# A hybrid mLSTM / attention / expert layer on one core: the products of each weight tile ordered by its high and low part

## The chip, the core and the metric

The kernel runs on one core of a Trainium2 chip. Its engines are TensorE (PE in the profile, with PEld for its weight loads), VectorE (DVE), ScalarE (ACT), GpSimd (POOL) and SyncE (SP), which issues most of the transfers. The metric is the device time of one execution in microseconds.

## The reference, cut to what matters

One layer for 256 latent tokens and 256 context tokens, width 2048, in float32:

```
h, hc   = modulate(rmsnorm(x)), modulate(rmsnorm(ctx))         # shifts and scales from c @ w_mod
q,k,v,z,gates,qa,ka,va,ga,gb = split(h @ w_in + b_in)          # the same for hc
y_m     = mLSTM in both directions (8 heads x 128), gated by z
y_d     = differential attention (8 heads)
x       = x + g1 * ((sig(ga) * (y_m @ w_pa) + sig(gb) * (y_d @ w_pb)) @ w_out)
h2      = modulate(rmsnorm(x))
s       = (h2 @ w_pq) . sub_keys   ->   top 16 of 16 x 16 for each of 8 heads   ->   idx, softmax g
act     = gelu(h2 . expert_u[idx])                             # 16384 experts
x       = x + g2 * sum(g * act * expert_v[idx])
out     = rmsnorm(x) * final_norm_w
```

## The kernel before, in words

All large products run in a rounded float32 format (`F32R`). To keep float32 accuracy each operand is split in two parts: a high part, the operand cast to that format, and a low part, the operand less its high part. A product of two operands is then three: high by high, activation-high by weight-low, activation-low by weight-high. `PASS` lists the three as pairs (part of the first operand, part of the second); index 0 is the high part and 1 the low one.

Weights come in tiles of 128 x 1024 (512 KB). `stage` brings one: a transfer into `raw` on SP's queue (line 117), a cast to `hi` on ACT (line 133) and a subtraction to `lo` (line 136) on DVE, or, in part of the kernel, every fourth one on POOL. The three tiles of each kind go round in rings of three buffers, and staging runs two to three tiles ahead (`look`). `take()` hands the next pair `hl = (hi, lo)` to its user. The users of the pairs are these:

- `token_part` (line 278): token-major blocks, where the activations are stationary and the weights move, 512 columns a product. Four token tiles (latent and context: `vm`, `va`) or two (`zm`, the output projection from `mgT`). Eight tiles make a block.
- `chan_part` (line 289): channel-major blocks, where the weights are stationary and 256 tokens move. With `n` = 2 both latent and context tokens (`hL`, `hC`; four accumulators: `km`, `ka`), with `n` = 1 the latent ones (two accumulators of two halves: `qa`, `qm`, gates, branch projections from `yT` and the like, and the query projection from `h`).
- `u_pair` (lines 1225 to 1228; both its products stand in the profile as line 93, the helper `mp_`): the expert stage, 256 tiles of `expert_u`. For each of eight chunks one product of `hi` with both parts of h2 (512 columns), and one of `lo` with its high part (256 columns), both into `s`.

The accumulators `acc` of the projections come from a pool of four PSUM buffers. A block that is done is emptied at once by ACT or DVE (lines 490, 500, 615, 665 and so on), and the next block's accumulator in the same buffer waits for that. Between blocks, `pump` advances generators with the other work: conv, mLSTM, attention, top-16 search, gate maps, lists of experts. In the expert stage, the two results of a pair are reduced on DVE (line 1634) and activated on ACT (line 1635), ahead of later casts in these engines' own order.

Last comes the sum over rows of `expert_v`. Some rows are used as float32 directly (groups of 32 tokens, `v<-vraw,w`), others are split (`split`, lines 1524 and 1526) and multiplied in `v_part`:

```
def v_part(hl, ins, t, hf_):
    for sa, sb in PASS:
        for c in range(2):
            mp_(out_acc[t][hf_ * 2 + c], lhsT=ins[sa], rhs=hl[sb][:, c * 512:(c + 1) * 512],
                start=False, stop=False, skip_group_check=True)
```

Products issued by `mm` are placed by a scheduler, which follows the order of the code where operands are ready by its own reckoning and moves others forward otherwise. Those issued by `mp_` keep the order of the code. On the chip each engine runs its fixed list in order.

Of the kernel before, what the change touches and what calls it, by code (L numbers as in the profile page):

```python
# [31 lines left out]
P = 128  # L32
D = 2048
T = 256
# [52 lines left out]
def build(tc, a, dump=None):  # L87
    nc = tc.nc
    mm = nc.tensor.matmul


    def mp_(*args, **kw):
        tc.keep_in_program_order(mm(*args, **kw))  # L93
# [21 lines left out]
    def load(src, pool, bufs, queue=nc.sync):  # L115
        r = pool.tile([P, 1024], F32, name="raw", tag="raw", bufs=bufs)
        d = queue.dma_start(r, src)  # L117
        if by_four[0]:
            tc.keep_in_program_order(d)
        return r  # L120
# [40 lines left out]
    def take():  # L161
        while len(ahead) < look[0]:
            src = next(todo, None)
            ahead.append(None if src is None else stage(src))
        return ahead.pop(0)
# [45 lines left out]
    def m_tile():  # L211
        return psM.tile([P, 512], F32, name="m", tag="m")
# [19 lines left out]
        return t if tok is None else t[:, tok * P:(tok + 1) * P]  # L232


    PASS = ((0, 0), (0, 1), (1, 0))
    ALL = (0, 1, 2, 3)
    back = []

# [13 lines left out]
    def pump(rate, ahead=2, beside=0):  # L252
        for i, (q, r) in enumerate(((front, ahead), (back, rate), (side, beside))):
            credit[i] += r if q else 0
            while credit[i] > 0.99:
                credit[i] -= 1
                step(q)
# [14 lines left out]
            step(back)  # L272

    def token_part(acc, hl, kp, lhs, first, last):
        for ti in range(len(acc)):
            for k2 in range(2):
                for i, (sa, sb) in enumerate(PASS):
                    mm(acc[ti], lhsT=lhs(sa, ti, 2 * kp + k2), rhs=hl[sb][:, k2 * 512:(k2 + 1) * 512],  # L278
                       start=first and k2 == 0 and i == 0, stop=last and k2 == 1 and i == 2)

    def chan_part(acc, hl, kp, rhs, n, first, last):

        for c in range(4):
            for k2 in range(2):
                k = 2 * kp + k2
                for i, (sa, sb) in enumerate(PASS):
                    for g in range(n):
                        w = (c if n == 1 else g) % 2
                        mm(acc[c][:, g * T:(g + 1) * T],  # L289
                           lhsT=hl[sb][:, k2 * 512 + c * P:k2 * 512 + (c + 1) * P], rhs=rhs(sa, g, k),  # L290
                           start=first and k2 == 0 and i == 0 and w == 0,
                           stop=last and k2 == 1 and i == 2 and w == 1, skip_group_check=True)

    def h_lhs(s, t, k):
        return hT(s, t // 2, k, t % 2)
# [7 lines left out]
    def token_block(lhs, n, done, *rate):  # L303
        acc = [acc_tile() for _ in range(n)]
        for kp in range(8):
            token_part(acc, take(), kp, lhs, kp == 0, kp == 7)
            pump(*rate)
        finish(done, acc)
# [4 lines left out]
    def chan_block(nk, rhs, n, done, *rate):  # L313
        acc = [acc_tile() for _ in range(2 * n)]
        view = acc if n == 2 else [half(acc, c) for c in range(4)]
        for kp in range(nk):
            chan_part(view, take(), kp, rhs, n, kp == 0, kp == nk - 1)
            pump(*rate)
        finish(done, acc)
# [47 lines left out]
    def mod_evac(k, ps):  # L367
        r4 = st.tile([P, T], F32, name="r4", tag="r4", bufs=2)
        nc.vector.tensor_copy(r4, ps[:, 0:T])
        yield  # L370
        pc = m_tile()
        for s in range(2):
            mm(pc[:, 2 * s:2 * s + 2], lhsT=r4[:, s * P:(s + 1) * P], rhs=sel4, start=True, stop=True)
        m = mod1[k]
        for s in range(2):
            nc.vector.tensor_scalar(m[:, s, :], pc[:, 2 * s:2 * s + 2], b1c[:, s, k:k + 1], float(s),
                                    op0=OP.add, op1=OP.add)
        nc.vector.tensor_scalar(m[:, 1, :], m[:, 1, :], nwc[:, 0, k:k + 1], None, op0=OP.mult)
        yield
# [31 lines left out]
    def vm_part(kp):  # L411
        token_part(vm_acc, take(), kp, h_lhs, kp == 0, kp == 7)
# [7 lines left out]
    part = 0  # L420
    ready = [0]
    for k in range(KT):
# [6 lines left out]
        ps = m_tile()  # L429
        for kp in range(4):  # L430
            w = load(a["w_mod1"][k, kp], stx, MOD_BUFS)
            for k4 in range(4):
                mm(ps[32 * k4:32 * k4 + 32, 0:T], lhsT=s1[:, 4 * kp + k4, :], rhs=w[:, k4 * T:(k4 + 1) * T],  # L433
                   start=kp == 0, stop=kp == 3, skip_group_check=True)
# [6 lines left out]
        g = mod_evac(k, ps)  # L441
# [608 lines left out]
    h2hl = [h2p.tile([P, 2 * T], F32R, name=f"h2_{k}") for k in range(KT)]  # L1050
    h2 = [[t[:, s * T:(s + 1) * T] for t in h2hl] for s in range(2)]
# [66 lines left out]
    def top16(src, vals, idx):  # L1118
        for r in range(2):
# [3 lines left out]
            if r == 0:  # L1123
# [6 lines left out]
    tv, ti = ([tk.tile([P, 16, 16], d, name=n, tag=f"{n}{t}", bufs=1) for t in range(2)] for n, d in  # L1130
              (("tv", F32), ("ti", U32)))
# [84 lines left out]
    def u_pair(i1, pace):  # L1216
        pss = []
        for e in range(2):
            ps = psS.tile([P, 2, T], F32, name="s", tag="s")
            flat = ps.rearrange("p s t -> p (s t)")  # L1220
            for hf_ in range(2):
                hl = take()
                for kk in range(8):
                    k = hf_ * 8 + kk
                    w = slice(kk * P, (kk + 1) * P)
                    mp_(flat, lhsT=hl[0][:, w], rhs=h2hl[k], start=k == 0, stop=False, skip_group_check=True)
                    mp_(ps[:, 1], lhsT=hl[1][:, w], rhs=h2[0][k], start=False, stop=k == 15, skip_group_check=True)
                pump(pace[0])
            pss.append(ps)
        return pss  # L1230
# [245 lines left out]
    n = P - N_LIST + 1  # L1476
# [52 lines left out]
    def halves(src, n, name, bufs, pool=None):  # L1529
        pool = pool or vst  # L1530
        r = [pool.tile([P, n], F32R, name=f"{name}{s}", tag=f"{name}{s}", bufs=bufs) for s in range(2)]
        nc.scalar.copy(r[0], src)
        nc.vector.tensor_tensor(r[1], src, r[0].bitcast(F32), op=OP.subtract)
        return r
# [36 lines left out]
    def next_item(n):  # L1571
        fetch(n)
        return [(raw, weights_of(kind, ins)) for (kind, _), (raw, ins) in
                zip(ITEMS[n], [fetched.pop(0) for _ in ITEMS[n]])]
# [75 lines left out]
# [5 lines that stand above are left out]
# [26 lines left out]
    with tc.If(rest > 0):  # L1681
        with tc.For_i(0, N_LIST, 1) as i:
            col_ = av.tile([P, 1], F32, name="ocol", bufs=1)
            nc.sync.dma_start(col_, over_dram[:, bass.ds(i, 1)])
            for t in range(2):
                ag = av.tile([P, 2 * P], F32, name="oag", bufs=1)
                nc.sync.dma_start(ag, ag_dram[bass.ds(i * P + P, P), 2 * t * P:2 * (t + 1) * P])
                w = ag[:, 0:P]
                nc.vector.scalar_tensor_tensor(w, ag[:, 0:P], col_, ag[:, P:2 * P], op0=OP.mult, op1=OP.mult)
                ins = halves(w, P, "o", 1, av)  # L1690
                for c in range(4):
                    raw = av.tile([P, 512], F32, name="oraw", bufs=1)
                    nc.sync.dma_start(raw, FULL[bass.ds(i * P, P), c * 512:(c + 1) * 512])
                    hl = halves(raw, 512, "r", 1, av)
                    for sa, sb in PASS:
                        mm(out_acc[t][c], lhsT=ins[sa], rhs=hl[sb], start=False, stop=False, skip_group_check=True)
# [35 lines left out]
    last = next_item(N_LAST)  # L1732
# [9 lines left out]
    last = next_item(N_LAST + 1)  # L1742
# [4 lines left out]
    last = next_item(N_LAST + 2)  # L1747
# [75 lines left out]
```

## Time and profile before

| | |
|---|---|
| median of 3 runs | 2292.78 us (2292.44 to 2295.87) |
| the profiled execution | 2298.06 us, span 2296.4 us |
| PE busy | 2170.8 us (95%) |
| DVE, ACT, POOL busy | 66%, 44%, 37% |
| granted TensorE clock, mean | 0.98 |
| first and last product with `expert_u` | 1169.7 and 2045.6 us |

A profile row of an instruction has its start and duration in microseconds, its engine, line and operation, what it writes and reads by the program's names, the shape, and in brackets the idle time of the engine before it with what ended it. A row of a group has the busy time, the mean of one in nanoseconds and the idle time ahead of the group's instructions. The duration of a product contains its way through the array, so the spacing of products is read from their starts. The span falls into: modulation and first blocks (to about 160 us), projections with mLSTM and attention beside them (to about 960), output and query projections (to 1170), the expert stage (to 2046), and the rows of V.

### The profile page before, as it was taken

Reading aid. Unit: us, or ns where it says so; the run is one execution under the profiler, and the core shown is the slowest. Engines: PE = TensorE matmul, PEld = TensorE weight load, DVE = VectorE, ACT = ScalarE, POOL = GpSimd, SP = SyncE. Lnnn points to the kernel's source line nnn. Section 1 sums busy time; section 2 is a strip of 40 time slices with the busy share of each in tenths; the row PEclk is TensorE's granted clock in tenths of the full one; section 3 lists DMA queues with packets and bytes.
Section 4 is the critical chain, followed back from the end, with each engine's and each line's share of the span. In section 5 each row is a group of like instructions: output and inputs, shape, how many; then the busy total and the mean of one; then the engine's idle time right before and its main releaser. Section 6 shows DMA issues by size and latency. Waiting matters only on the chain.

```text
span 2296.4 us, 36937 instructions
## 1 busy us (share of the span) xinstructions
PE 2170.8 (95%) x14088; PEld 1865.0 (81%) x14088; DVE 1513.6 (66%) x2739; ACT 1021.3 (44%) x1629; POOL 838.3 (37%) x822
## 2 busy tenths in 40 slices
PE   6999999999999999998998999989999899989994
PEld 3668988999899999977997879877888787656662
DVE  3448883667886767755689766767997444335554
ACT  3232232233565844444444668854454343324332
POOL 2132210226354301001224557741223125457674
PEclk9999999999999999998999999999999999999997
DMA  9968973876556588865555557896656768899997
GB/s 380 344 216 299 331 248 130 287 239 195 146 154 195 150 275 284 280 208 178 175 175 170 192 173 212 229 246 208 211 181 237 279 205 291 325 351 412 386 376 298
DMA packets 235172, 566.77 MB, mean 247 GB/s; under 512 B 85058, under 2 KB 118643, under 8 KB 220912
## 3 DMA queue, kind: packets, MB, share of 16 engines
q1 hardware_dynamic: 153888, 339.34, 44.9%
q0 software_dynamic: 46256, 207.47, 25.0%
q10 hardware_dynamic: 34848, 17.57, 2.7%
q8 instruction: 111, 1.82, 0.3%
q14 instruction: 69, 0.57, 0.1%
HBM read 520.14 MB, written 38.93 MB: 243 GB/s over the span
## 4 chain that ended last, share of the span: by engine, by line
PE 76%; DVE 9%; DMA 6%; issue 3%; ACT 2%; POOL 2%; SPq 0%; ACTq 0%; POOLq 0%; DVEq 0%
PE s L93 24%; PE acc L289 23%; PE acc L278 11%; PE v L93 9%; PE g L93 3%; DVE lo L136 3%; DMA raw<-expert_u 2%; PE m L433 1%; ACT hi L133 1%; PE m L278 1%; DMA raw<-w_mod 1%; POOL lo L136 1%; DMA ag<-ag_dram,idxG 1%; DMA raw<-w_in 1%; DVE most L1257 1%
## 5 line engine op out<-in xcount | busy, mean ns | idle before, releaser
L133 ACT CAST hi<-raw 128x1024 fp32r<-128x1024 f32 x528 | 552.0, 1048 | 855.1 <-PE acc L289 276.8
L136 DVE TENSOR_TENSOR lo<-raw,hi 128x1024 fp32r<-128x1024 f32 x457 | 575.5, 1262 | 297.7 <-ACT hi L133 292.2
L93 PE MATMUL s<-h,hi 128*128 128x512 f32 x2048 | 744.8, 405 | 8.3 <-ACT hi L133 8.3
L93 PE MATMUL s<-h,lo 128*128 128x256 f32 x2048 | 581.5, 284 | 21.1 <-DVE lo L136 13.5
L93 PEld LDWEIGHTS s<-h,hi 128*128 128x128 f32 x2048 | 390.2, 191 | 102.5 <-ACT hi L133 10.5
L289 PE MATMUL acc<-hL,hi 128*128 128x256 f32 x2048 | 421.6, 286 | 0.0
L93 PEld LDWEIGHTS s<-h,lo 128*128 128x128 f32 x2048 | 392.7, 192 | 28.4 <-DVE lo L136 18.0
L289 PEld LDWEIGHTS acc<-hL,hi 128*128 128x128 f32 x2048 | 342.3, 193 | 1.4
L136 POOL TENSOR_TENSOR lo<-raw,hi 128x1024 fp32r<-128x1024 f32 x71 | 181.3, 2553 | 424.7 <-ACT hi L133 397.0
L289 PE MATMUL acc<-hL,lo 128*128 128x256 f32 x1024 | 291.9, 286 | 5.0 <-DVE lo L136 4.8
L289 PEld LDWEIGHTS acc<-hL,lo 128*128 128x128 f32 x1024 | 197.5, 193 | 6.5 <-DVE lo L136 5.9
L117 POOL DMA_DIRECT2D raw<-w_mod x128 | 67.9, 531 | 299.6 <-DVE raw L522 277.6
L522 DVE SCALAR_TENSOR_TENSOR raw<-raw,cr 128x1024 f32<-128x1024 f32 x128 | 154.4, 1219 | 32.4 <-DMA raw<-w_mod 17.9
L1247 POOL TENSOR_SCALAR o<-iota,i1T,gT 128x128 f32<-128x128 f32 x128 | 143.4, 1128 | 75.6 <-PE g L93 42.0
L1526 DVE TENSOR_TENSOR lo<-vraw,hi 128x1024 fp32r<-128x1024 f32 x68 | 82.7, 1226 | 87.6 <-ACT hi L1524 60.8
L1510 POOL DMA_INDIRECT vraw<-expert_v,idxV x96 | 108.6, 1131 | 76.3 <-PE v L93 30.0
L289 PE MATMUL acc<-hC,hi 128*128 128x256 f32 x512 | 134.0, 283 | 0.0
L1634 DVE TENSOR_REDUCE act<-s 128x256 f32<-128x512 f32 x126 | 86.3, 685 | 61.6 <-PE s L93 57.1
L1510 POOL DMA_INDIRECT ag<-ag_dram,idxG x96 | 104.8, 1092 | 41.7 <-issue 35.3
L1524 ACT CAST hi<-vraw 128x1024 fp32r<-128x1024 f32 x68 | 70.8, 1048 | 98.0 <-PE v L93 53.8
L278 PE MATMUL acc<-hi,hL 128*128 128x512 f32 x320 | 111.0, 406 | 0.5 <-ACT hi L133 0.5
L93 PE MATMUL v<-hi,l 128*128 128x512 f32 x384 | 107.5, 398 | 1.4 <-issue 1.2
(431 smaller groups left out, 3641.4 us busy)
## 6 DMA issues: line engine op xcount, KB each, us to landing
raw<-expert_u SPq DMA_DIRECT2D x256, 512.0 KB
raw<-w_in SPq DMA_DIRECT2D x176, 512.0 KB
raw<-w_mod POOLq DMA_DIRECT2D x128, 512.0 KB
raw<-w_mod SPq DMA_DIRECT2D x64, 512.0 KB
raw<-w_out SPq DMA_DIRECT2D x32, 512.0 KB
raw<-w_pq SPq DMA_DIRECT2D x32, 512.0 KB
ag_dram<-gates SPq DMA_DIRECT2D x32, 512.0 KB
ag_dram<-act ACTq DMA_DIRECT2D x126, 128.0 KB
```

Of the source, the lines that this page charges most:

```text
L93: tc.keep_in_program_order(mm(*args, **kw))
L117: d = queue.dma_start(r, src)
L133: nc.scalar.copy(h, r)
L136: (nc.vector if shared[0] else nc.gpsimd).tensor_tensor(l, r, h.bitcast(F32), op=OP.subtract)
L278: mm(acc[ti], lhsT=lhs(sa, ti, 2 * kp + k2), rhs=hl[sb][:, k2 * 512:(k2 + 1) * 512], start=first and k2 == 0 and i == 0, stop=last and k2 ...
L289: mm(acc[c][:, g * T:(g + 1) * T], lhsT=hl[sb][:, k2 * 512 + c * P:k2 * 512 + (c + 1) * P], rhs=rhs(sa, g, k), start=first and k2 == 0 and ...
L522: product = nc.vector.scalar_tensor_tensor(r, r, 1.0, cr, op0=OP.mult, op1=OP.mult, accum_out=part[:, h, i:i + 1])
L1247: (nc.gpsimd if i % 2 else nc.vector).tensor_scalar(o2[:, i], iota, cols[:, i:i + 1], factor[:, i:i + 1], op0=OP.is_equal, op1=OP.mult)
L1510: tc.keep_in_program_order(nc.gpsimd.indirect_dma_start(out=out, out_offset=None, in_=src, in_offset=bass.IndirectOffsetOnAxis(ap=idx[:, b ...
L1524: nc.scalar.copy(h, raw)
L1526: nc.vector.tensor_tensor(l, raw, h.bitcast(F32), op=OP.subtract)
L1634: nc.vector.reduce_sum(act[:, e], ps.rearrange("p s t -> p t s"), axis=AX.X)
```

## The change

`PASS` is put in the order high by high, low by high, high by low, and cut in two by the weight's part: `BY_PART`. In `token_part` and `chan_part` that cut becomes the outermost loop, so that all products of a tile with `hi` come first and all with `lo` after them. In `u_pair` one loop of eight pairs becomes two loops of eight. In `v_part` nothing is edited, but its `PASS` has the new order, so the low part of the rows comes last. The number of products, loads and transfers is the same.

```diff
-    PASS = ((0, 0), (0, 1), (1, 0))
+    PASS = ((0, 0), (1, 0), (0, 1))
+    BY_PART = PASS[:2], PASS[2:]
...
     def token_part(acc, hl, kp, lhs, first, last):
-        for ti in range(len(acc)):
-            for k2 in range(2):
-                for i, (sa, sb) in enumerate(PASS):
-                    mm(acc[ti], lhsT=lhs(sa, ti, 2 * kp + k2), rhs=hl[sb][:, k2 * 512:(k2 + 1) * 512],
-                       start=first and k2 == 0 and i == 0, stop=last and k2 == 1 and i == 2)
+        for part in BY_PART:
+            for ti in range(len(acc)):
+                for k2 in range(2):
+                    for sa, sb in part:
+                        mm(acc[ti], lhsT=lhs(sa, ti, 2 * kp + k2), rhs=hl[sb][:, k2 * 512:(k2 + 1) * 512],
+                           start=first and k2 == 0 and (sa, sb) == (0, 0), stop=last and k2 == 1 and sb == 1)
...
     def chan_part(acc, hl, kp, rhs, n, first, last):
-        for c in range(4):
-            for k2 in range(2):
-                k = 2 * kp + k2
-                for i, (sa, sb) in enumerate(PASS):
-                    for g in range(n):
+        for part in BY_PART:
+            for c in range(4):
+                for k2 in range(2):
+                    k = 2 * kp + k2
+                    for sa, sb in part:
+                        for g in range(n):
...
                 for kk in range(8):
                     k = hf_ * 8 + kk
-                    w = slice(kk * P, (kk + 1) * P)
-                    mp_(flat, lhsT=hl[0][:, w], rhs=h2hl[k], start=k == 0, stop=False, skip_group_check=True)
-                    mp_(ps[:, 1], lhsT=hl[1][:, w], rhs=h2[0][k], start=False, stop=k == 15, skip_group_check=True)
+                    mp_(flat, lhsT=hl[0][:, kk * P:(kk + 1) * P], rhs=h2hl[k], start=k == 0, stop=False,
+                        skip_group_check=True)
+                for kk in range(8):
+                    k = hf_ * 8 + kk
+                    mp_(ps[:, 1], lhsT=hl[1][:, kk * P:(kk + 1) * P], rhs=h2[0][k], start=False, stop=k == 15,
+                        skip_group_check=True)
```

First place: PE at the first tile of the expert stage (`h_0` to `h_7` are the chunks of h2, `hi` and `lo` the tile's parts), before:

```order
L93 MATMUL s<-h_0_10160,hi 128x512
L93 MATMUL s<-h_0_10160,lo 128x256
L93 MATMUL s<-h_1_10161,hi 128x512
L93 MATMUL s<-h_1_10161,lo 128x256
L93 MATMUL s<-h_2_10162,hi 128x512
L93 MATMUL s<-h_2_10162,lo 128x256
```

and PE in the changed program at the same tile:

```order
L93 MATMUL s<-h_4_10164,hi 128x512
L93 MATMUL s<-h_5_10165,hi 128x512
L93 MATMUL s<-h_6_10166,hi 128x512
L93 MATMUL s<-h_7_10167,hi 128x512
L93 MATMUL s<-h_0_10160,lo 128x256
L93 MATMUL s<-h_1_10161,lo 128x256
L93 MATMUL s<-h_2_10162,lo 128x256
```

The first product with `lo` was the second of sixteen and is now the ninth.

Second place: PE at the end of the first `km` block, whose four accumulators are `acc_1752` to `acc_1755`; the next block begins with `acc_2264`, which takes the buffer of `acc_1752`. Before:

```order
L289 MATMUL acc_1755<-hC03_116,hi_2061 128x256
L289 MATMUL acc_1755<-hL03_108,lo_2063 128x256
L289 MATMUL acc_1755<-hC03_116,lo_2063 128x256
L289 MATMUL acc_1755<-hL13_112,hi_2061 128x256
L289 MATMUL acc_1755<-hC13_120,hi_2061 128x256
L289 MATMUL acc_2264<-hL00_105,hi_2121 128x256
L289 MATMUL acc_2264<-hC00_113,hi_2121 128x256
```

and in the changed program (line 292 is line 289 before), a little ahead of the block's end:

```order
L292 MATMUL acc_1752<-hL03_108,lo_2063 128x256
L292 MATMUL acc_1752<-hC03_116,lo_2063 128x256
L292 MATMUL acc_1753<-hL03_108,lo_2063 128x256
L292 MATMUL acc_1753<-hC03_116,lo_2063 128x256
L292 MATMUL acc_1753<-hL03_108,lo_2063 128x256
L292 MATMUL acc_1753<-hC03_116,lo_2063 128x256
L292 MATMUL acc_1754<-hL03_108,lo_2063 128x256
L292 MATMUL acc_1754<-hC03_116,lo_2063 128x256
L292 MATMUL acc_1754<-hL03_108,lo_2063 128x256
L292 MATMUL acc_1754<-hC03_116,lo_2063 128x256
```

Four products on `acc_1755` and one transpose follow, and then the next block. The last product on `acc_1752` stood 36 products ahead of the block's end and now stands 12 ahead of it.

More of the change, by code (lines that the diff above doesn't have):

```diff
@@ L274, in token_part @@
     def token_part(acc, hl, kp, lhs, first, last):
-        for ti in range(len(acc)):
-            for k2 in range(2):
-                for i, (sa, sb) in enumerate(PASS):
-                    mm(acc[ti], lhsT=lhs(sa, ti, 2 * kp + k2), rhs=hl[sb][:, k2 * 512:(k2 + 1) * 512],
-                       start=first and k2 == 0 and i == 0, stop=last and k2 == 1 and i == 2)
-    def chan_part(acc, hl, kp, rhs, n, first, last):
-        for c in range(4):
-            for k2 in range(2):
-                k = 2 * kp + k2
-                for i, (sa, sb) in enumerate(PASS):
-                    for g in range(n):
[L288 to L292, printed above, removed]
+        for part in BY_PART:
[4 more added lines that the diff above has]
+                           start=first and k2 == 0 and (sa, sb) == (0, 0), stop=last and k2 == 1 and sb == 1)
+    def chan_part(acc, hl, kp, rhs, n, first, last):
+        for part in BY_PART:
[4 more added lines that the diff above has]
+                        for g in range(n):
+                            w = (c if n == 1 else g) % 2
+                            mm(acc[c][:, g * T:(g + 1) * T],
+                               lhsT=hl[sb][:, k2 * 512 + c * P:k2 * 512 + (c + 1) * P], rhs=rhs(sa, g, k),
+                               start=first and k2 == 0 and (sa, sb) == (0, 0) and w == 0,
+                               stop=last and k2 == 1 and sb == 1 and w == 1, skip_group_check=True)
     def h_lhs(s, t, k):
```

## The prediction

> **What bounds the kernel now.** I read the page first: the span, the busy time of each engine, the slices and the chain that ended last.
>
> ```profile
> span 2296.4 us, 36937 instructions
> PE 2170.8 (95%) x14088; PEld 1865.0 (81%) x14088; DVE 1513.6 (66%) x2739; ACT 1021.3 (44%) x1629; POOL 838.3 (37%) x822
> DMA  9968973876556588865555557896656768899997
> PE 76%; DVE 9%; DMA 6%; issue 3%; ACT 2%; POOL 2%; SPq 0%; ACTq 0%; POOLq 0%; DVEq 0%
> ```
>
> TensorE carries 76% of the chain. No product is added or removed, so the change can act only on the 125.6 us in which PE is idle, on the spacing of products, and on the clock. DVE's 9% is what PE waits for most. DMA is busy at 0.8 or more only in the first slices and in the last eight (from about 1840 us).
>
> Then the groups by line, for the idle time of PE ahead of each kind of product (the last column):
>
> ```profile
> L93 PE MATMUL s<-h,hi 128*128 128x512 f32 x2048 | 744.8, 405 | 8.3 <-ACT hi L133 8.3
> L93 PE MATMUL s<-h,lo 128*128 128x256 f32 x2048 | 581.5, 284 | 21.1 <-DVE lo L136 13.5 <-POOL lo L136 6.7 <-issue 0.8
> L289 PE MATMUL acc<-hL,lo 128*128 128x256 f32 x1024 | 291.9, 286 | 5.0 <-DVE lo L136 4.8
> L289 PE MATMUL acc<-h,hi 128*128 128x256 f32 x512 | 96.7, 289 | 6.1 <-ACT hi L133 5.0 <-ACT h L1096 1.1
> L278 PE MATMUL acc<-lo,mgT 128*128 128x512 f32 x128 | 51.3, 400 | 0.9 <-DVE lo L136 0.9
> L93 PE MATMUL v<-lo,l 128*128 128x512 f32 x192 | 60.6, 396 | 1.1 <-DVE lo L1526 0.5 <-issue 0.5
> ```
>
> The wait for a weight tile's low part is 21.1 us in the expert stage (`s`, line 93), about 6 us in the projections (5.0 and 0.9) and 1.1 us for the rows of V. The waits for a high part (8.3 and 6.1 us) are not addressed directly. Next, who waits for `lo`, and the six longest of these waits in the timeline of PE (idle time in brackets):
>
> ```profile
>   PE s L93: 20.1, 15
> ...
> 1536.24 0.38 PE L93 MATMUL s<-h,lo 128*128 128x256 f32 x1 [2.87 <-DVE lo L136]
> 1545.37 0.58 PE L93 MATMUL s<-h,lo 128*128 128x256 f32 x1 [2.28 <-DVE lo L136]
> 1793.62 0.58 PE L93 MATMUL s<-h,lo 128*128 128x256 f32 x1 [1.70 <-POOL lo L136]
> 1898.42 0.39 PE L93 MATMUL s<-h,lo 128*128 128x256 f32 x1 [2.66 <-DVE lo L136]
> 1986.39 0.58 PE L93 MATMUL s<-h,lo 128*128 128x256 f32 x1 [1.99 <-POOL lo L136]
> 2018.19 0.39 PE L93 MATMUL s<-h,lo 128*128 128x256 f32 x1 [1.98 <-POOL lo L136]
> ```
>
> Fifteen waits make 20.1 us; these six make 13.5 us of it, the other nine 6.6 us. None is a standing shortage: 256 tiles pass, and fifteen are late.
>
> **The expert stage: how much later the low part is needed.** The spacing of products is read from starts in the timeline: this stage, then the query projection (products of 256), then the output projection (products of 512).
>
> ```profile
> 1503.26 0.39 PE L93 MATMUL s<-h,hi 128*128 128x512 f32 x1
> 1503.49 0.28 PE L93 MATMUL s<-h,lo 128*128 128x256 f32 x1
> 1503.61 0.39 PE L93 MATMUL s<-h,hi 128*128 128x512 f32 x1
> ...
> 1156.23 0.40 PE L289 MATMUL acc<-h,hi 128*128 128x256 f32 x2
> 1156.47 0.28 PE L289 MATMUL acc<-h,lo 128*128 128x256 f32 x1
> 1156.59 0.40 PE L289 MATMUL acc<-h,hi 128*128 128x256 f32 x2
> ...
> 1012.39 0.39 PE L278 MATMUL acc<-lo,mgT 128*128 128x512 f32 x1
> 1012.62 0.63 PE L278 MATMUL acc<-hi,mgT 128*128 128x512 f32 x2
> 1013.09 0.39 PE L278 MATMUL acc<-lo,mgT 128*128 128x512 f32 x1
> ```
>
> A high product takes 0.23 us and a low one 0.12 us. Before, the low part is needed 0.23 us after the high part; now after eight high products, 8 x 0.23 = 1.86 us. That is 1.63 us more cover for each tile. Of the six long waits each gives back 1.63 us (9.8 us), and the nine short ones, 6.6 us together and none of them over 1.60, vanish: 16.4 us. Three things take some back. After the wait at 1536 the next tile's high part is itself late, so 1.6 us turn into a wait for `hi`; one of the short waits at 1778 goes the same way (0.8 us); and the last two lie where DMA is at 0.8 to 0.9, for which I give back half of 3.2 us. That leaves 12.4; I take 12. The low end counts the cover once for each of the five places (1536 and 1545 as one): 5 x 1.63 = 8. The high end is the whole 20.
>
> One wait shows the chain that feeds these tiles (timeline of four engines):
>
> ```profile
> 1787.65 0.69 DVE L1634 TENSOR_REDUCE act<-s 128x256 f32<-128x512 f32 x1 [2.32 <-PE s L93]
> 1788.38 0.63 ACT L1635 ACTIVATE act<-act 128x512 f32<-128x512 f32 x1 [4.90 <-DVE act L1634]
> 1790.04 1.99 ACT L133 CAST hi<-raw 128x1024 fp32r<-128x1024 f32 x2 [1.03 <-issue]
> 1791.13 0.79 PE L93 MATMUL s<-h,hi 128*128 128x512 f32 x1 [3.52 <-ACT hi L133]
> 1791.21 2.35 POOL L136 TENSOR_TENSOR lo<-raw,hi 128x1024 fp32r<-128x1024 f32 x1 [12.56 <-ACT hi L133]
> ```
>
> The last line cannot begin before the cast ends, and PE begins the high products at that same moment. So POOL's 2.35 us are covered to 1.86 us in the new order, and nearly not at all in the old. The 3.52 us before it stay: the cast stands behind the reduction and the activation of the finished pair, in ACT's own order. The same row shows what is next late when a low part is no longer late: the next high part. The high tile's own buffer comes free after two thirds of its products (0.94 us earlier), so its cast may start earlier; I count nothing for that, and put it into a rival.
>
> **Spacing.** Alternating, a pair takes 0.35 us. Runs would take 0.233 + 0.12 = 0.353 by the query and output projections' rows. 2048 pairs x 0 to 3 ns is 0 to 6 us lost; I take 3.
>
> **Projections.** Their low part is needed after 16 products of 0.12 us (1.9 us) for 256-token blocks, after 32 for 512-token ones, so waits of 2.0 us like the two below go nearly whole. Of 6 us I take 4 (ends 0 and 6). Against it stands a wait that the order creates. A block with four accumulators finishes them now all in its last third: the first is complete 12 products x 0.12 = 1.44 us before the block's end, where it was 36 products, 4.3 us. The next block's first product needs that accumulator emptied:
>
> ```profile
> 298.61 0.69 ACT L615 ACTIVATE xp<-acc,bic 128x512 f32<-128x512 f32 x1 [0.75 <-PE acc L289]
> 205.39 1.22 DVE L522 SCALAR_TENSOR_TENSOR raw<-raw,cr 128x1024 f32<-128x1024 f32 x1
> 206.54 1.29 DVE L490 TENSOR_TENSOR vxl<-acc,brow 128x512 f32<-128x512 f32 x2
> 568.70 2.29 DVE L136 TENSOR_TENSOR lo<-raw,hi 128x1024 fp32r<-128x1024 f32 x1
> ...
> L136 DVE TENSOR_TENSOR lo<-raw,hi 128x1024 fp32r<-128x1024 f32 x457 | 575.5, 1262 | 297.7 <-ACT hi L133 292.2
> ```
>
> Emptying takes 0.69 us, so 0.75 us are spare; an instruction of 1.22 us ahead of it on DVE makes a wait of at most 0.5 us. Eight such boundaries (vm to qa) cost 0 to 4 us by this row, and far more by the row of 2.29 us (the slower rival). I take 2. Blocks with two accumulators alternate buffers and have over 12 us: nothing.
>
> **Rows of V.** Each half row block has six products per token tile; the low rows are needed after four instead of two, 0.47 us more cover, against 1.1 us of idle time: 1 us (0 to 1). The gate weights' low part is needed two products earlier. The code makes both parts of it ahead of the row's own cast and subtraction on the same engines, so a block whose rows are there has its weights: 0; were it late, 0.47 us for a block.
>
> **The clock.** Windows around some waits (us, then busy time by engine, then granted clock, DMA share and GB/s):
>
> ```profile
> 571.04 0.39 PE L289 MATMUL acc<-hL,lo 128*128 128x256 f32 x1 [2.03 <-DVE lo L136]
> ...
> 572.40:575.80 3.40, 3.31 (x16) 3.01 (x15) 3.40 (x7) 0.34 (x1) 2.41 (x4) 0.50 0.52 171
> 1797.80:1985.40 187.60, 179.95 (x1045) 147.75 (x1043) 81.60 (x91) 68.84 (x73) 67.05 (x43) 1.00 0.74 253
> 2019.60:2023.00 3.40, 3.40 (x17) 2.03 (x19) 1.76 (x3) 1.17 (x2) 2.19 (x2) 0.50 0.89 320
> ```
>
> A wait of 2.0 us at 571 is followed by 3.4 us at half clock, and so is the one at 2018; the 188 us between, with one such wait (1898), ran at full clock. 3.4 us at half speed with PE busy throughout cost 1.7 us. Waits of 2 us that shrink to 0.4 should take their windows with them. I count three such windows gone, 5 us; the ends are 0 and 12 us (one 1.7 us for each of the seven long waits shown).
>
> The Trainium skill, page "TensorE: Matmul & The Clock Gate", section "Why this matters for your kernels", asks for no idle gap over about 3 us between bursts, since an idle window drops the clock to half. By that rule the two-microsecond waits would cost no clock, this term would be 0 and the time 2281; the rows show half clock after a wait of 2.0 us, and the measurement decides.
>
> **Sum.** 12 + 4 + 1 + 5 gained, 3 + 2 lost: 17 us. The profiled execution took 2298.06 us (span 2296.4), the median of the three runs is 2292.78, so the profiled one is 5.3 us long; I take the 17 us off the median: 2276.
>
> **Rivals.**
> *More.* High tiles come free 0.94 us earlier, casts run ahead, and the waits for `hi` (8.3 and 6.1 us) shrink with their half-clock windows. For it: the cast is what PE waits for 3.52 us at 1791. Against: there it is held by the pair's activation, not by a buffer. If most of that 14 us goes, 12 us more are gained: 2264.
>
> *No change.* Each tile still needs copy, cast and subtraction in turn; PE that no longer waits for `lo` waits for `hi`. Then only the low end of the expert stage holds: 8 + 1 gained, and spacing and boundaries at 6 + 2 lost, clock unchanged: 2292. For it: the wait for `hi` at 1791 directly precedes one for `lo`, and DMA is near full at the end.
>
> *Slower.* The boundaries of the eight four-accumulator blocks: if DVE stands in a subtraction of 2.29 us plus a 1.22 us product when the first accumulator completes, PE waits 2.29 + 1.22 + 0.69 - 1.44 = 2.8 us, and a half-clock window follows (1.7 us): 8 x 4.5 = 36 us, less the 19 us gained elsewhere: 2310. It decides from 2.4 us a boundary, wait and clock together. For it: DVE runs back to back at 206 us. Against: 2.29 is rare, the mean of that group of 457 is 1.26 us, and ACT empties half of the blocks.
>
> That the change does nothing is excluded for the expert stage, where the order is kept as written; in the projections the listing shows it too.
>
> **Chances.** Forecast 0.50 (its own range 2270 to 2286); more 0.20 (2258 to 2270); no change 0.18; slower 0.12. A measurement of this kernel tells about 0.2% (4.6 us) from no change: 2288.2 to 2297.4. Faster is 0.50 + 0.20 = 0.70, within 0.18, slower 0.12. The range leaves out the slower case and part of the better one: 2262 to 2297.
>
> **What would show it.** In the profile after: idle time ahead of `s<-h,lo` down from 21.1 to under 6 us; ahead of `s<-h,hi` not over 13; ahead of `acc<-hL,lo` under 2; a run of eight low products at 0.12 us each; waits of PE for the emptying lines (490, 500, 615, 665) under 4 us in sum; fewer windows at half clock. I am wrong if the wait for `hi` grows by what the wait for `lo` loses, or if PE idles at the first product of a block.

## The result, and the profile after

The changed kernel takes 2278.98 us (median of 7 runs, 2272.16 to 2285.87); the kernel before, run beside it, 2292.44 us (7 runs). The ratio is 0.9948, with a 95% interval of 0.9927 to 0.9968: 13.5 us or 0.5% faster. In a later comparison (below) the ratio was 0.9938 (0.9918 to 0.9958).

The two profiled executions stand further apart than the medians: span 2270.4 us after, the shortest of its runs, against 2296.4 before, which was a long one. Of these 26.0 us about half is not in the medians, so I compare terms, and test each against the profiles of the experiments.

First the head of the page of the changed kernel:

```profile
span 2270.4 us, 37003 instructions
PE 2156.6 (95%) x14088; PEld 1865.9 (82%) x14088; DVE 1520.4 (67%) x2739; ACT 1021.6 (45%) x1629; POOL 838.9 (37%) x822
```

As many products as before, 14.2 us less of PE's busy time and 11.8 us less of its idle time. Now both kernels cut at the same four events: the first product of the `km` block, the first and the last product with `expert_u`, the end. The columns are start and end, length, busy time (and instructions) of PE, PEld, DVE, ACT and POOL, then granted clock, DMA share and GB/s. First the kernel before:

```profile
0.00:208.40 208.40, 184.74 (x1160) 126.23 (x1161) 102.71 (x214) 64.99 (x86) 50.08 (x83) 0.99 0.84 312
208.40:1169.81 961.41, 938.69 (x6879) 891.60 (x6878) 686.13 (x1239) 414.84 (x677) 248.83 (x335) 0.99 0.66 217
1169.81:2045.83 876.02, 834.61 (x4947) 712.10 (x4946) 597.28 (x1044) 451.91 (x728) 379.37 (x262) 0.98 0.72 228
2045.83:2296.40 250.57, 212.72 (x1106) 135.10 (x1104) 127.45 (x244) 89.56 (x138) 160.00 (x144) 0.94 0.92 372
```

and the changed one:

```profile
0.00:213.16 213.16, 186.23 (x1161) 127.74 (x1161) 105.59 (x217) 66.86 (x87) 48.07 (x85) 0.98 0.83 308
213.16:1168.28 955.12, 936.15 (x6880) 890.91 (x6879) 683.26 (x1240) 411.17 (x676) 250.04 (x333) 0.99 0.66 218
1168.28:2024.92 856.64, 824.55 (x4947) 713.45 (x4946) 602.66 (x1040) 452.62 (x729) 386.68 (x261) 0.99 0.72 231
2024.92:2270.40 245.48, 209.66 (x1107) 133.84 (x1105) 128.94 (x245) 90.92 (x138) 154.11 (x143) 0.94 0.94 383
```

The third column is the one to read. The expert stage is 19.4 us shorter. The projections are 6.3 us shorter, but the first stage is 4.8 us longer, which the prediction had not thought of. The rows of V are 5.1 us shorter here; over the profiles of all kernels below that stretch varies from 241.8 to 254.1 us with no visible relation to the edits, so none of it is credited to the change.

The idle time of PE ahead of each group, against the rows of before:

```profile
L93 PE MATMUL s<-h,hi 128*128 128x512 f32 x2048 | 529.7, 401 | 18.4 <-ACT hi L133 18.4
L93 PE MATMUL s<-h,lo 128*128 128x256 f32 x2048 | 288.4, 284 | 2.8 <-DVE lo L136 1.8 <-POOL lo L136 0.8
L292 PE MATMUL acc<-hL,lo 128*128 128x256 f32 x1024 | 177.0, 286 | 0.7 <-DVE lo L136 0.7
L93 PE MATMUL v<-lo,l 128*128 128x512 f32 x192 | 60.3, 395 | 0.0
```

In the expert stage the wait for the low part fell from 21.1 to 2.8 us, and the wait for the high part rose from 8.3 to 18.4: 18.3 us removed, 10.1 us come back under another name, 8.2 us won in waits. (The busy time of these groups is lower because of how ends of products in a run are counted; the spacing is read from starts, below.) The waits for high parts are few and long. Five of them, in the timeline of PE:

```profile
1532.58 1.71 PE L93 MATMUL s<-h,hi 128*128 128x512 f32 x6 [2.08 <-ACT hi L133]
1548.72 3.78 PE L93 MATMUL s<-h,hi 128*128 128x512 f32 x8 [4.58 <-ACT hi L133]
1774.40 2.12 PE L93 MATMUL s<-h,hi 128*128 128x512 f32 x8 [2.45 <-ACT hi L133]
1784.88 2.11 PE L93 MATMUL s<-h,hi 128*128 128x512 f32 x8 [3.52 <-ACT hi L133]
1969.08 3.78 PE L93 MATMUL s<-h,hi 128*128 128x512 f32 x8 [3.52 <-ACT hi L133]
```

They make 16.2 of the 18.4 us, and stand in the same stretches in which the kernel before waited for low parts (1536 to 1561, 1777 to 1794, 1984). The cover of 1.63 us was enough to hide the subtraction, and then the cast, one step up the same chain, is what is late.

Two stretches, 1515 to 1565 and 1765 to 1800 us, hold most of this exchange. In them PE waited 16.4 us for high and low parts together before, and waits 16.6 us now: nothing is won there. In the rest of the stage the sum fell from 13.0 to 4.5 us (in a second profile of the changed kernel the two sums are 16.1 and 7.4). In the kernel before, the DMA share of these two stretches (the last but one figure of a row) was already 0.89 and 0.97, and casts in the first of them waited for their tiles:

```profile
1515.00:1565.00 50.00, 41.00 (x221) 34.70 (x220) 30.09 (x40) 18.34 (x29) 10.96 (x6) 0.93 0.89 236
1765.00:1800.00 35.00, 27.56 (x137) 22.33 (x137) 12.52 (x11) 10.47 (x12) 14.00 (x10) 0.90 0.97 389
...
1535.37 1.04 ACT L133 CAST hi<-raw 128x1024 fp32r<-128x1024 f32 x1 [2.56 <-DMA raw<-expert_u]
...
1545.85 1.04 ACT L133 CAST hi<-raw 128x1024 fp32r<-128x1024 f32 x1 [3.31 <-DMA raw<-expert_u]
```

After the change ACT's timeline shows two different reasons for the late casts:

```profile
1547.62 1.04 ACT L133 CAST hi<-raw 128x1024 fp32r<-128x1024 f32 x1 [6.61 <-DMA raw<-expert_u]
...
1773.30 1.04 ACT L133 CAST hi<-raw 128x1024 fp32r<-128x1024 f32 x1 [4.47 <-DMA raw<-expert_u]
...
1782.12 0.63 ACT L1641 ACTIVATE act<-act 128x512 f32<-128x512 f32 x1 [3.88 <-DVE act L1640]
1782.78 0.90 ACTq L1645 DMA_DIRECT2D ag_dram<-act  x2
1783.78 2.24 ACT L133 CAST hi<-raw 128x1024 fp32r<-128x1024 f32 x2 [1.03 <-issue]
```

The first two casts stand idle until the tile itself has landed. The last one does not wait for a transfer: it stands in ACT's list behind the activation of the pair that PE has just finished, and behind the issues of that activation's two writes. The order that the description of the kernel gives, the activation ahead of later casts, is rare: ACT's list has three or more casts of the next pair ahead of the activation in 54 of 63 pairs, in the kernel before as now. None stand ahead of it in two pairs now, this one and the one before the wait at 1969, and in one pair before, the one before the wait of 3.52 us at 1791. Both reasons became theories to test.

### The profile page after: what moved, and what is told of

Read it like the earlier page. It is cut to its first block, busy times and chain, and to the rows that moved or that the text cites. A ratio compares the mean times of both kernels' runs of the same rounds, so it can differ in the third digit from the quotient of the medians.

```text
span 2270.4 us, 37003 instructions
## 1 busy us (share of the span) xinstructions
PE 2156.6 (95%) x14088; PEld 1865.9 (82%) x14088; DVE 1520.4 (67%) x2739; ACT 1021.6 (45%) x1629; POOL 838.9 (37%) x822
## 3 DMA queue, kind: packets, MB, share of 16 engines
q8 instruction: 111, 1.82, 0.3%
## 5 line engine op out<-in xcount | busy, mean ns | idle before, releaser
L93 PE MATMUL s<-h,hi 128*128 128x512 f32 x2048 | 529.7, 401 | 18.4 <-ACT hi L133 18.4
L93 PEld LDWEIGHTS s<-h,hi 128*128 128x128 f32 x2048 | 371.6, 191 | 92.9 <-ACT hi L133 21.0
L292 PE MATMUL acc<-hL,hi 128*128 128x256 f32 x2048 | 334.1, 285 | 0.0
L93 PEld LDWEIGHTS s<-h,lo 128*128 128x128 f32 x2048 | 280.9, 192 | 26.8 <-DVE lo L136 3.9
L292 PEld LDWEIGHTS acc<-hL,hi 128*128 128x128 f32 x2048 | 293.3, 192 | 1.8 <-ACT kA L669 0.3
L93 PE MATMUL s<-h,lo 128*128 128x256 f32 x2048 | 288.4, 284 | 2.8 <-DVE lo L136 1.8
L292 PE MATMUL acc<-hL,lo 128*128 128x256 f32 x1024 | 177.0, 286 | 0.7 <-DVE lo L136 0.7
L292 PEld LDWEIGHTS acc<-hL,lo 128*128 128x128 f32 x1024 | 151.3, 193 | 2.1 <-DVE lo L136 0.9
L292 PE MATMUL acc<-hC,hi 128*128 128x256 f32 x512 | 124.7, 283 | 0.0
L93 PE MATMUL v<-vraw,w 128*32 128x512 f32 x640 | 81.0, 632 | 20.9 <-DVE w L1551 13.1
```

Source lines behind the costliest of these rows:

```text
L292: mm(acc[c][:, g * T:(g + 1) * T], lhsT=hl[sb][:, k2 * 512 + c * P:k2 * 512 + (c + 1) * P], rhs=rhs(sa, g, k), start=first and k2 == 0 and ...
```

## The experiments

All are timed in five rounds beside the kernel before. The experiments on the first stage, the queues and the gathers ran on one chip and all others on another; the changed kernel was not run beside the first of these, so there I compare by the ratio to the kernel before. Waits are the sums of PE's idle time ahead of `s<-h,hi` and `s<-h,lo`.

### Which part of the change pays

The kernel before, with only the new loops of `u_pair`:

```diff
                 for kk in range(8):
-                    mp_(flat, lhsT=hl[0][:, w], rhs=h2hl[k], ...)
-                    mp_(ps[:, 1], lhsT=hl[1][:, w], rhs=h2[0][k], ...)
+                    mp_(flat, lhsT=hl[0][:, kk * P:(kk + 1) * P], rhs=h2hl[k], ...)
+                for kk in range(8):
+                    k = hf_ * 8 + kk
+                    mp_(ps[:, 1], lhsT=hl[1][:, kk * P:(kk + 1) * P], rhs=h2[0][k], ...)
```

> The kernel before, with only the expert stage in the new order (eight high products, then eight low). Theory (cover in the expert stage): nearly the whole gain is here, 10 to 14 us under the kernel before (about 2280), idle time of PE ahead of s<-h,lo falls from 21.1 to about 3 us and ahead of s<-h,hi rises from 8.3 to about 18 us; the projections' waits stay (5.0 us ahead of acc<-hL,lo). Rival (the projections or the rows of V bring half of it): 4 to 7 us under (2285 to 2288), with the same rows in the expert stage.

And the kernel before, with only the new loops of `token_part` and `chan_part` (the second and third hunks of the diff; `PASS` for the rows of V stays as it was):

> The kernel before, with only the projections (token and channel blocks) in the new order; the expert stage and the rows of V keep the old one. Theory: the low-part waits of the projections go (5.0 us to under 1), but the first stage ends later, as in the changed kernel (first product of the km blocks at 213 instead of 208 us), so the sum is within 3 us of the kernel before (2289 to 2295). Rival: the later end of the first stage was chance in one profile; then it is 3 to 6 us faster (2286 to 2289).

The first took 2276.46 us, ratio 0.9935 (0.9913 to 0.9957); the second 2289.91 us, ratio 1.0000 (0.9987 to 1.0014). The whole gain comes from the expert stage. Groups of the first, then of the second, then two stretches of the second (up to the first `km` product, and from there to the expert stage):

```profile
L93 PE MATMUL s<-h,hi 128*128 128x512 f32 x2048 | 531.3, 402 | 17.9 <-ACT hi L133 17.9
L93 PE MATMUL s<-h,lo 128*128 128x256 f32 x2048 | 289.1, 284 | 4.8 <-DVE lo L136 4.0 <-POOL lo L136 0.8
```

```profile
L93 PE MATMUL s<-h,hi 128*128 128x512 f32 x2048 | 743.1, 404 | 6.9 <-ACT hi L133 6.9
L93 PE MATMUL s<-h,lo 128*128 128x256 f32 x2048 | 581.3, 284 | 22.6 <-DVE lo L136 12.9 <-POOL lo L136 9.5
L292 PE MATMUL acc<-hL,lo 128*128 128x256 f32 x1024 | 175.7, 284 | 0.9 <-DVE lo L136 0.9
```

```profile
0.00:211.19 211.19, 183.62 (x1161) 126.20 (x1162) 105.63 (x217) 67.19 (x87) 48.05 (x85) 0.98 0.84 311
211.19:1166.40 955.21, 932.74 (x6879) 887.44 (x6878) 684.06 (x1240) 411.03 (x676) 249.42 (x333) 0.99 0.67 218
```

The exchange of waits (low down, high up) comes with `u_pair` alone and is absent without it. The projections do what was foreseen (the wait ahead of `acc<-hL,lo` is 0.9 us, the stretch 6.2 us shorter than the 961.41 of before), and lose 2.8 us ahead of that stretch.

### Half the cover

The changed kernel, with `u_pair` in runs of four high and four low products, twice for each tile. The low part is then needed after four high products (0.92 us) instead of eight (1.85 us):

```diff
-                for kk in range(8):
-                    mp_(flat, ...)
-                for kk in range(8):
-                    mp_(ps[:, 1], ...)
+                for half_ in range(2):
+                    for kk in range(4 * half_, 4 * half_ + 4):
+                        mp_(flat, ...)
+                    for kk in range(4 * half_, 4 * half_ + 4):
+                        mp_(ps[:, 1], ...)
```

> The changed kernel, but in the expert stage four high products, four low, four high, four low: the low part is needed 0.93 us after the high one, between 0.23 before and 1.86 in the changed kernel; the high tile comes free 0.47 us ahead of the low one instead of 0.94. Theory (cover): the fifteen waits for the low part shrink by 0.7 us each, so the idle time ahead of s<-h,lo is about 11 us, and the time lies between, 2283 to 2288. Rival (it is enough that the low part is not the second product, or the earlier release of the high tile brings the gain): idle ahead of s<-h,lo under 5 us, time as the changed kernel (2276 to 2282).

2283.28 us, ratio 0.9973 (0.9956 to 0.9991), between the two kernels (the changed one took 2275.42 us on this chip):

```profile
L93 PE MATMUL s<-h,hi 128*128 128x512 f32 x2048 | 574.2, 402 | 11.0 <-ACT hi L133 11.0
L93 PE MATMUL s<-h,lo 128*128 128x256 f32 x2048 | 331.0, 284 | 13.3 <-DVE lo L136 9.9 <-POOL lo L136 3.0
```

With 0, 0.69 and 1.63 us more cover than in the old order the low waits are 21.1, 13.3 and 2.8 us and the high ones 8.3, 11.0 and 18.4: a dose and its response, in both columns. The other profiles bear it out: 22.6 us of low waits in the second kernel with the old loops, 2.1 to 6.7 us in all eight with the loops of eight and the scheduler's own order of casts. That the cover is the mechanism is shown.

### The first stage in the old order

The changed kernel, with `vm_part` and `zm_part` (the blocks of the first stage) calling a copy of the old `token_part`:

```diff
-        token_part(vm_acc, take(), kp, h_lhs, kp == 0, kp == 7)
+        first_order(vm_acc, take(), kp, h_lhs, kp == 0, kp == 7)
...
-        token_part(zm_acc, take(), kp, h_lhs, kp == 0, kp == 7)
+        first_order(zm_acc, take(), kp, h_lhs, kp == 0, kp == 7)
```

> The changed kernel with the first stage's blocks (vm and zm of the modulation stage's neighbours, up to the first km product) in the old order, all else as changed. In the traces so far the first km product starts at 207 to 208 us in the two kernels with the old projection order and at 211 to 213 us in the three with the new one. Theory A, the new order delays the first stage: the first km product comes back to 207 to 209 us and the time falls by 3 to 5 us below the changed kernel's (from about 2279 to about 2275). Theory B, the difference of the first stage is chance from run to run or comes from the km blocks behind it: the first km product stays at 211 to 213 us and the time stays at 2279.

2273.96 us, ratio 0.9905 (0.9877 to 0.9932). The last product of the modulation with the weights and the first product of `km`, in the kernel before, in the changed one and in this one:

```profile
142.43 1.93 PE L433 MATMUL m<-raw,s 128*32 128x256 f32 x32
...
208.40 0.28 PE L289 MATMUL acc<-hL,hi 128*128 128x256 f32 x1
```

```profile
119.70 0.61 PE L376 MATMUL m<-sel,r 128*128 128x2 f32 x4 [1.82 <-DVE r L372]
...
153.19 0.62 PE L436 MATMUL m<-raw,s 128*32 128x256 f32 x2
...
213.16 0.28 PE L292 MATMUL acc<-hL,hi 128*128 128x256 f32 x1
```

```profile
141.44 1.93 PE L443 MATMUL m<-raw,s 128*32 128x256 f32 x32
...
207.18 0.28 PE L299 MATMUL acc<-hL,hi 128*128 128x256 f32 x1
```

The first `km` product starts at 207.2 to 208.4 us in all five kernels with the old order in the first stage, and at 211.2 to 215.8 us in all eight with the new one. So a loss of some 5 us there (3 to 9) is real and comes from these two blocks. Their products stand between those of the modulation, and the scheduler, which counts operands as ready by its own reckoning, places the two kinds differently: the modulation's last weights are used 10 us later, with a wait of 1.82 us for DVE on the way. All eight kernels with the new order have that wait, none of the five with the old one. In the total time the gain is likely, not shown: this ratio and the changed kernel's overlap at their ends (0.9932 against 0.9927, and 0.9918 in its repeat).

### Why the high part is late: the queues

The changed kernel, with the writes of the gate maps moved from SP's queue to POOL's (32 in all; eight of them stand among the tiles' issues at 1515 to 1540 us):

```diff
-            tc.keep_in_program_order(nc.sync.dma_start(rows[:, i:i + 16, w], g[:, j:j + 16, :]))
+            tc.keep_in_program_order(nc.gpsimd.dma_start(rows[:, i:i + 16, w], g[:, j:j + 16, :]))
```

> The changed kernel with the eight writes of the gate maps (ag_dram<-gates, line 1262) issued on POOL's queue instead of SP's, where they stand between the issues of expert_u tiles at 1525 to 1550 us. The changed kernel waits 18.4 us for high parts in the expert stage, 7.0 us of it in two waits in that window. Theory A, the queue: those two waits go, the idle time ahead of the high products falls to about 11 us and the time by 5 to 8 us (half-clock windows with it). Theory B, the load of all transfers together makes the tiles land late, whichever queue issues them: 18 us stay and the time stays the same within 2 us.

2283.09 us, ratio 0.9942 (0.9921 to 0.9963), as the changed kernel. The wait at 1532 is gone; the one at 1549 is there as before, and a new one for a low part comes 27 us later:

```profile
1545.04 3.78 PE L93 MATMUL s<-h,hi 128*128 128x512 f32 x8 [4.73 <-ACT hi L133]
...
1572.10 1.22 PE L93 MATMUL s<-h,lo 128*128 128x256 f32 x8 [2.02 <-DVE lo L136]
```

Together 21.1 us of waits, against 21.2 in the changed kernel. One wait went with the queue's load and others of the same sum came, so SP's queue did not set the sum. This edit together with the old first stage gave no more:

> The changed kernel with the first stage in the old order and the gate-map writes on POOL's queue. If both theories A of these parts hold, the gains add: 8 to 13 us below the changed kernel, 2266 to 2271. If only the first stage's holds 2275, if neither 2279.

2278.80 us, ratio 0.9905 (0.9879 to 0.9932): the same ratio as the old first stage alone. Against the kernel with only the queue edit, on the same chip, it is 4.3 us shorter, which speaks for the first stage's 5 us once more, but their runs overlap (2269.86 to 2282.49 against 2276.86 to 2288.02).

Then the first gathers of V's rows, which in the changed kernel go out eight together from 1757 us, spread out:

```diff
                     rows.append(stage_rows(*b))
-                    yield
+                    for _ in range(3):
+                        yield
```

> The changed kernel with the first gathers of V's rows (vraw<-expert_v) spread over the expert stage: groups of 1 to 2 instead of 3 and 5 together. In the changed kernel tiles of expert_u land 9 to 12 us after their issue during the burst of eight (from 1757 us), 3.7 us otherwise, and PE waits 4.5 us for high parts in three waits there. Theory A, the burst slows the landings: those waits shrink to under 1.5 us, and the time falls by 3 to 4 us. Theory B, the waits come from the order of casts behind the pair's activation: they stay, and the time is the same within 2 us.

2278.40 us, ratio 0.9911 (0.9886 to 0.9935); against the changed kernel no difference that this can tell. The four waits of 1769 to 1785 have gone, and two stand in their place. The first is behind a pair's activation on ACT again, the second behind a cast that waited for its tile:

```profile
1782.37 3.53 PE L93 MATMUL s<-h,hi 128*128 128x512 f32 x8 [2.99 <-ACT hi L133]
...
1812.26 3.78 PE L93 MATMUL s<-h,hi 128*128 128x512 f32 x8 [5.07 <-ACT hi L133]
```

```profile
1811.16 1.04 ACT L133 CAST hi<-raw 128x1024 fp32r<-128x1024 f32 x1 [9.64 <-DMA raw<-expert_u]
```

Spread out, the gathers did not stop tiles from landing late: PE waits 8.3 us in this stretch, against 7.9 in the changed kernel, and 23.7 us in all.

### Why the high part is late: ACT's order

The changed kernel, with a pair's reduction and activation written after the first two tiles of the next pair:

```diff
-        pss = u_pair(i1, pace)
+        pss = u_pair(i1, pace, late.pop() if late else None)   # runs it after its first two tiles
```

> The changed kernel, with the reduction, activation and writing of a pair's results issued only after the first of the next pair's two expert tiles. Theory (what PE waits for now is a cast that stands behind the finished pair's activation in ACT's order): the idle time ahead of s<-h,hi falls from 18.4 to about 8 us, and the time is 6 to 10 us under the changed kernel (2269 to 2273). Rival (what it waits for is the landing of the raw tile, with three buffers): the idle time stays at 15 to 20 us and the time within 3 us of the changed kernel.

2281.31 us, ratio 0.9958 (0.9942 to 0.9974), with 19.8 us of waits for high parts: not faster than the changed kernel, which took 2275.42 us on this chip. At first I took this for evidence against ACT's order. It was not: the trace still shows the activation ahead of the casts at the place in question,

```profile
1784.16 0.63 ACT L1646 ACTIVATE act<-act 128x512 f32<-128x512 f32 x1 [4.32 <-DVE act L1645]
...
1785.81 1.99 ACT L133 CAST hi<-raw 128x1024 fp32r<-128x1024 f32 x2 [1.03 <-issue]
```

because the scheduler, and not the code, sets the order of casts and activations. So the order was then fixed:

```diff
-        nc.scalar.copy(h, r)
+        c = nc.scalar.copy(h, r)
+        if by_four[0]:                       # in the expert stage
+            tc.keep_in_program_order(c)
...
-        nc.scalar.activation(act, act, AF.Gelu)
+        tc.keep_in_program_order(nc.scalar.activation(act, act, AF.Gelu))
```

> The changed kernel with ACT's casts and the pair's activation in the expert stage kept in the order of the code. In the listing of the changed kernel three casts of the next pair's tiles stand ahead of a pair's activation in 47 of 64 pairs, but none in the pairs whose next tile waits 3.52 us (at 1784.88 and 1969.08); here it is two in all pairs but the last. Theory A, these waits are made by ACT's order: both go (7 us of the 18.4 us of waits for high parts, to about 11) and with them up to two windows at half clock; 5 to 10 us under the changed kernel. Theory B, the tile itself lands late there: a wait of 2 to 3.5 us stays at both places, and the time stays within 2 us.

2297.45 us, ratio 1.0027 (1.0013 to 1.0041): 22 us slower than the changed kernel on the same chip (its repeat, below), which neither theory gave. The groups, one of the new waits with what DVE did there, and ACT's casts around the pair whose successor had waited 3.52 us:

```profile
L93 PE MATMUL s<-h,hi 128*128 128x512 f32 x2048 | 533.6, 403 | 18.0 <-ACT hi L133 17.9
L93 PE MATMUL s<-h,lo 128*128 128x256 f32 x2048 | 288.5, 284 | 23.9 <-DVE lo L138 21.0 <-POOL lo L138 3.0
```

```profile
1498.73 1.22 PE L93 MATMUL s<-h,lo 128*128 128x256 f32 x8 [4.00 <-DVE lo L138]
...
1489.27 6.85 DVE L1265 TENSOR_REDUCE most<-gates 128x32 f32<-128x1024 f32 x6
```

```profile
1803.67 1.05 ACT L133 CAST hi<-raw 128x1024 fp32r<-128x1024 f32 x1 [2.85 <-DMA raw<-expert_u]
...
1811.46 1.05 ACT L133 CAST hi<-raw 128x1024 fp32r<-128x1024 f32 x1 [2.85 <-DMA raw<-expert_u]
1812.41 0.62 ACT L1643 ACTIVATE act<-act 128x512 f32<-128x512 f32 x1
```

On the two places theory A was right: the activation now stands behind the casts (1812.41), and no wait of 3.52 us is left after either pair. The waits in the stretch that begins at 1765 us fell from 7.9 to 5.3 us. On the time it was wrong. The fixed order upset the rest of the plan: at 1489 us DVE's subtraction stands behind six reductions in a row for the gate maps (6.85 us), and 21 us of waits for low parts are back, about as much as the kernel is slower. And what is left in the stretch itself are casts that each end a wait for their tile, 3.9 us apart, while PE uses up a tile in 2.8 us: there the transfers set the pace.

The last two kernels ran on one chip with this one. The old first stage with the fixed order and the activation after two tiles:

> The changed kernel with the first stage in the old order, and with ACT's casts and the pair's activation kept in order, the activation after two tiles of the next pair: four casts stand ahead of it in nearly all pairs. If theory A on ACT's order holds and the first stage's 5 us are there too: 10 to 15 us under the changed kernel, with under 11 us of waits for high parts. If only the first stage counts: 3 to 5 us under it.

2282.58 us, ratio 0.9968 (0.9955 to 0.9981); 11.1 us of waits for high parts and 18.6 for low ones. The high waits fell as theory A said, and the low ones took it back: 7 us slower than the changed kernel, where 3 to 15 us faster was expected. And the changed kernel once more:

> The changed kernel itself on the chip of the two others, so that they are compared with it directly. Its waits for high parts should be 18 us again with 3.5 us at two places, and its ratio to the kernel before 0.993 to 0.997.

2275.42 us, ratio 0.9938 (0.9918 to 0.9958), with 18.6 and 4.9 us. No kernel here is shown to beat the changed one; the one with the old first stage (0.9905) may.

## Why the prediction was right, point by point

The forecast was 17 us; the runs give 13.5 (15 in the later comparison). The mechanism and the place were right. Several sizes were not: the waits gave less, the spacing lost nothing, and the projections gained nothing in sum. That these errors nearly cancelled is luck.

**Expert stage, 12 us from waits.** It was 8.2 us (29.4 to 21.2 us for both kinds), the low end. The step that failed is what was taken back. For the waits that turn into waits for `hi` I had counted 1.6 and 0.8 us, and half of 3.2 us near the end; 10.1 us came back, so "`hi` not over 13" missed with 18.4, and the sign of being wrong, `hi` growing by what `lo` loses, came more than half true. The places were taken the wrong way round. The prediction read the DMA row as 0.8 or more only in the first slices and the last eight, and gave back half for the last two of the six waits for that. But the slices from 1435 to 1550 us in that row stand at 8 and 9, and the stretch from 1765 to 1800, at 0.97, is hidden in slices of 6 and 7. In these two stretches nothing was won, while the waits at 1898 and 2018 went nearly whole. The signs `s<-h,lo` under 6 (2.8) and `acc<-hL,lo` under 2 (0.7) held. The cover removes a wait only where the chain of copy, cast and subtraction is late by a moment. Where the copy is late, the wait moves one step up that chain. The rival "no change" was half right: it named this exchange. "More" fell: high parts did not come earlier, because at the five long waits their casts stand behind a tile's landing or a pair's activation, not behind a buffer. Over both profiles of the changed kernel the sum of waits is 21.2 and 23.5 us.

**Spacing, 3 us lost.** No loss is seen. A tile (eight pairs) in the last third of the stage takes 2.82 us before and 2.79 after. In the middle of the stage before it took 2.77, the 0.35 a pair that I had read at 1503; I took one place for all. Over all tiles at full clock, without a wait and with no other product between, the mean is 2.839 us before (128 tiles) and 2.823 after (132): 256 x 0.016 = 4 us won between these two profiles. But the second experiment, which has the old loops, has 2.828 (126 tiles), so how much of the 4 us is the order's is not shown.

**The clock, 5 us.** In the expert stage the clock's records show 34.1 us at half speed before and 23.9 after: three windows of 3.4 us fewer, 5.1 us, as counted. But the new waits bring windows of their own, and not each of them: the eight high products after the wait of 2.45 us at 1774 and after the one of 3.52 us at 1784 ran at full clock, those after 3.52 us at 1969 at half. In the seven other profiles with the new loops of eight and the scheduler's own order of casts, the stage has 20.5 to 34.1 us at half clock, and 30.7 with the old loops in the second experiment, so the size of this term is not shown. On the rule from the Trainium skill that was weighed against it (page "TensorE: Matmul & The Clock Gate", section "Why this matters for your kernels", an idle gap over about 3 us): in the repeat of the changed kernel eight high products took 3.28 us instead of 2.0 after a shorter gap,

```profile
1772.43 3.28 PE L93 MATMUL s<-h,hi 128*128 128x512 f32 x8 [2.30 <-ACT hi L133]
```

so a gap of 2.3 us can go with half clock, as in the profile before, and one of 3.52 us need not.

Waits 8.2, clock 5.1 and spacing 4 make 17 of the 19.4 us by which the stage is shorter in these two profiles; 2 us are not traced to rows.

**Projections, 4 us won; boundaries, 2 us lost.** The low waits of the projections went nearly whole, and the stretch from `km` to the experts is 6 us shorter: 953 to 959 us in all eleven kernels with the new order there, 961 and 963 in the two with the old one. The boundaries cost nothing that shows: in the trace of the changed kernel no product waits for an emptying line, and weight loads do three times, 0.4 us in sum, so "slower" fell with its 2.4 us a boundary. The step missing was the first stage, where the order that the scheduler makes of two interleaved kinds of work lost some 5 us. The sum of both is 0 in the timed runs (the second experiment).

**Rows of V, 1 us.** The 1.1 us ahead of `v<-lo,l` went to 0.0; in the first experiment, with the old order of V's rows, it is 0.0 too, so the change is not what removed it.

## What to carry to other kernels

Ordering work by the operand that arrives last pays by the cover it gives, but only as far as the operand before it in the same chain is in time: ask, for each wait that goes, what the next earlier step was doing then, and look there for what comes back (here 10.1 of 18.3 us). In the two stretches of this kernel where tiles were already landing late, the new order only changed the name of the wait; everything was won in the rest. And where a scheduler places the work, an edit in one block moves others: compare the lengths of stages, not the waits alone, and look at the engine's order before believing that an edit to the code has changed it.

## What was not expected of the hardware

The same alternation of a 512-column and a 256-column product ran with two spacings in one execution, 2.77 and 2.82 to 2.83 us for eight pairs, for long stretches each. In runs of eight, 98 of the 132 tiles counted above took 2.79 us and none took less. What switches between the two was not tried.
